# A hybrid decoder block on one core: the last weights' sums in quarter pieces, convolution taps queued behind products, other accumulator banks in mixing

## The chip, the cores and the metric

The kernel runs on one core of one Trainium2 chip. The time is the device time of one execution in microseconds (us), and the smaller the better. All engines are named as the profile names them: PE is TensorE (matmuls), DVE is VectorE, ACT is ScalarE, POOL is GpSimd, and SP is SyncE, which here issues all transfers (DMAs). Each engine works through its own instructions in order, and waits where one of them needs something of another engine or a transfer.

## The reference

One layer of a hybrid decoder block on 512 tokens of 1024 channels, in float32:

```
h = rmsnorm(x, norm1_g)
z_glu, z_rx, z_rg, z_ga, z_gb = split(h @ w_in + b_in)      # widths 2048, 1280, 1280, 1024, 1024
u  = z_glu[:, :1024] * sigmoid(z_glu[:, 1024:])
u  = causal_depthwise_conv(u, conv_dw_w, 31 taps)
ya = silu(layernorm(u)) @ conv_w_out + conv_b_out
xb = causal_depthwise_conv(z_rx, lru_conv_w, 4 taps)
hb = rg_lru(xb)                                             # gates in 16 blocks of 80, linear recurrence
yb = (hb * gelu(z_rg)) @ lru_w_out
x  = x + (sigmoid(z_ga) * ya + sigmoid(z_gb) * yb) @ w_mix_out
h  = rmsnorm(x, norm2_g)
x  = x + (silu(h @ ffn_w1) * (h @ ffn_w3)) @ ffn_w2         # width 2816
out = rmsnorm(x, norm_f_g)
```

## The kernel before

**Numbers and products.** Every float32 operand of a matmul is split into a high and a low part, and a product is three matmuls (high by high, high by low, low by high) into one accumulator. Three large products (mixing, the SwiGLU input, `ffn_w2`) are done in a seven-product form on 2x2 quarters, which needs sums of quarters of the weights and of the activations, and saves one matmul in eight. The weight sums (`t1` to `t4`) are made on the chip and stored in DRAM ahead of their use.

**Stages.** The first norm and its transposes; the input projection in tiles of 128 columns, in the hand-written order `ORDER`; the products `yb` and `ya`; mixing (`mxr`, L880); the second norm and its transposes (`th`); the SwiGLU input products for k = 0 to 10, of which k = 2 to 7 are the seven-product form (`ffn_seven`, `fr`, L1060: seven products of 24 matmuls of 128x256) and the others direct (`f`, L468: 24 matmuls of 128x512 a tile); the output product (`or`, L880); the final norm.

**Weight chunks.** All weights come in a fixed list of chunks of 128x1024 (`wchunk`, `emit_chunk`). Each chunk takes a `raws` tile (`RAW = 4` of them) for SP's load and an `hls` tile (5) for its parts; ACT casts the high part (L124) and DVE or POOL subtracts to get the low one (L120). `weights(key)` emits the chunks up to four ahead (`AHEAD = 4`) of the one that PE asks for. So the load of a chunk is issued when the chunk four before it was converted.

**The sums of `ffn_w2`.** For k = 0 and 1, POOL makes them during the input projection in half-column pieces (`o_piece` inside `make_f_sums`): two loads into one of three `wsums` tiles, four 128x256 operations, one store. For k = 2 to 10, `out_sums` calls `make_sums(k)` (L287) at the points of `OUT_SUMS`: it takes two of the four `raws` tiles, loads 512 KB into each, has DVE do four 128x512 operations (`ows`, L120 and L294), and stores them to DRAM (`ot<-ows`, L298). Its only rule of order is that it stands behind `turned`, the end of the second norm.

**Activation sums of the output product.** `Sevenfold.pair` makes the sums of one output pair (`ous`, `os`, `oe`, `ov`) on ACT and DVE. `release(keep)` does the pairs that are waiting, all but the last `keep`. The high and low parts `u_` of the first three pairs lie in `wsums` tiles (`PIECES`).

**The taps.** `beside` is a generator: each step is one tap of the 31-tap convolution on DVE (`cv`, L627), into a bank of accumulator memory; after the taps come ACT's copies `u`, then the layer norm's mean (`lnmt`, `lnms`, `lnmp`). `run_beside(n)` takes n steps after each tile of the projection. `rg(j)` is the tile of `z_rg`: Gelu on ACT (L785), the product with the recurrence's state on DVE (L786), and the split `y`. `gates(j)` (L733) makes the recurrence's coefficients; its operation `xb` at L760 reads the last of a gate's two banks.

**Banks.** Accumulator memory has eight banks: six in the pool `psum` (`bank`) and two in `psum2` (`bank2`). A tile gets a bank when its last reader is done. In `Sevenfold.run`, r1, r2, r5 and later r3 come from `bank`, r7 from `bank2`.

**Order.** The program order within an engine is chosen by a scheduler from the dependences and the order of the code. `tc.issue_after(x)` puts what it encloses behind instruction x; `manual_schedule` keeps the order written.

Of the kernel before, what the change touches and what calls it, by code (L numbers as in the profile page):

```python
# [1 line left out]

# [11 lines left out]
P = 128  # L14
T = 512
# [17 lines left out]
RAW = 4  # L33
HL = 5
AHEAD = 4
WARM = 12

FEW, MANY = 32, 112
# [49 lines left out]
def tile_block(ctx, tc, a, out):  # L88
# [53 lines left out]
    def emit_chunk():  # L142
        key, src, kt, cols, where, lo, after = chunks[emitted[0]]
        emitted[0] += 1
        n = kt * cols
        raw = raws.tile([P, 1024], F32, tag="raw", name=f"raw_{key}")
        rv = raw[:, :n]
        if callable(src):
            src(raw)
        else:  # L150
            newest["load"] = nc.sync.dma_start(rv.rearrange("p (k n) -> p k n", k=kt), src).ins
# [167 lines left out]
    def f_chunk(n, k):  # L319
        def load(raw_t):  # L320
            if n[0] == "t":
                nc.sync.dma_start(raw_t, f_sums[k][:, IN_PLACE.index(n), :])
            else:
                for i, w_ in enumerate((w1, w3)):
                    nc.sync.dma_start(raw_t[:, i * T : (i + 1) * T].rearrange("p (k n) -> p k n", k=4), f_quarter(n, k, w_, 0, 4))

        wchunk(f"f{n}_{k}", load, 8, P, lo=vec)

    def make_f_sums():

        def f_piece(k, i, c):
            four = (w1, w3)[i].rearrange("p (h k) (e n) -> p h k e n", h=2, e=2)
            at = T * i + P * c
            halves = [four[:, h, c : c + 2, :, k * P : (k + 1) * P].rearrange("p k e n -> p e k n") for h in range(2)]
            return f"{k}_{i}_{c}", halves, f_sums[k][:, :, at : at + 256]

        def o_piece(k, c):
            four = outq.w.rearrange("p (h k) (e n) -> p h k e n", h=2, e=2)
            cs = slice(256 * c, 256 * c + 256)
            return f"o{k}_{c}", [four[:, h, k, :, cs] for h in range(2)], outq.all_sums[k][:, :, cs]

        todo = [f_piece(k, i, c) for k in SEVEN for i in range(2) for c in (0, 2)]
        todo += [o_piece(k, c) for k in range(OUT_EARLY) for c in range(2)]
        sums_due, stores_due = [], []
        n, next_at = 0, SUMS_AT
        while todo or sums_due or stores_due:  # L350
            if stores_due and (emitted[0] >= stores_due[0][0] or not (todo or sums_due)):
                stores_due.pop(0)[1]()
            if sums_due and n >= sums_due[0][0]:
                sums_due.pop(0)[1]()
            if todo and n >= next_at:
                next_at += SUMS_STEP - (n >= SUMS_DENSE)
                name, halves, dest = todo.pop(0)
                raw = wsums.tile([P, 1024], F32, tag="wsum", name=f"fws{name}")
                q = [raw[:, 256 * m : 256 * m + 256] for m in range(4)]
                with tc.issue_after(newest["load"]):  # L360
                    for h, src in enumerate(halves):
                        to = raw[:, h * T : h * T + T]
                        to = to.rearrange("p (e k n) -> p e k n", e=2, k=2) if len(src.shape) == 4 else to.rearrange("p (e n) -> p e n", e=2)
                        nc.sync.dma_start(to, src)

                def sums(raw=raw, q=q, dest=dest):
                    q11, q12, q21, q22 = q
                    with tc.issue_after(newest["sub"]):
                        sub(pool_e, q22, q22, q12)
                        sub(pool_e, q12, q12, q11)  # L370
                        pool_e.tensor_tensor(out=q11, in0=q22, in1=q11, op=ALU.add)
                        sub(pool_e, q21, q21, q11)

                    def stores():
                        with tc.issue_after(newest["load"]):
                            nc.sync.dma_start(dest, raw.rearrange("p (m n) -> p m n", m=4))
# [406 lines left out]
    def rg(j):  # L783
        ps = in_mm(RG + j)
        act.activation(ps, ps, AF.Gelu_apprx_tanh, bias=b_in(RG + j))  # L785
        vec.tensor_tensor(out=ps, in0=hs[j], in1=ps, op=ALU.mult)  # L786
        y.append(split(f"y{j}", ps, vec))

    f_sums_steps = make_f_sums()
# [45 lines left out]
    class Sevenfold:  # L835
# [20 lines left out]
        def pair(self, k, ua, va):  # L856

            n = self.name

            p_ = None  # L860
            if n == "o" and k < PIECES:
                both = wsums.tile([P, 1024], F32R, tag="wsum", name=f"{n}us{k}")
                p_ = both[:, :T], both[:, T:]
            u_ = split(f"{n}us{k}", ua, vec, p_)
# [17 lines left out]
        def run(self, sums, begun, end):  # L882
# [71 lines left out]
    def mix_end(second, plus, r1, r2, r7, third):  # L954
# [11 lines left out]
        with tc.manual_schedule(engines={ET.PE, ET.Activation, ET.DVE}):  # L966
# [27 lines left out]


    o7 = Sevenfold(outq)
    sums_of = iter(range(OUT_EARLY, KF))

    def out_sums(n):

        with tc.issue_after(turned):
            for _ in range(n):
                k = next(sums_of, None)
                if k is not None:
                    outq.make_sums(k)

    def ffn_out(j, p1, p3):
        s_ = shortt(f"si{j}")
        act.activation(s_, p1, AF.Silu)
        o7.tile(j, lambda cs, dst: vec.tensor_tensor(out=dst, in0=s_[:, cs], in1=p3[:, cs], op=ALU.mult))  # L1010

    first_two = [0, KF]
    wf = [(w_tiles(f"f1_{j}", ND, 0), w_tiles(f"f3_{j}", ND, 0)) for j in first_two]
# [37 lines left out]
    def ffn_seven(k):  # L1051
# [12 lines left out]

        def out_of(c, dst):
            act.activation(c[:, LO], c[:, LO], AF.Silu)
            vec.tensor_tensor(out=dst, in0=c[:, LO], in1=c[:, HI], op=ALU.mult)
# [5 lines left out]
        product(r2, "a12", "b21")  # L1073
        add(c11, r2, c11)
        out_of(c11, u_[:, LO])
        product(r3, "s4", "b22")
        product(r1, "s2", "t2", True)
        q = shortt(f"q_{k}")
# [13 lines left out]
        product(r1, "a22", "t4", True)  # L1092
        add(c21, r1, c21)
        out_of(c21, v_[:, LO])
        o7.uv.append((u_, v_))
        o7.waiting.append((k, u_, v_))

    for k in range(1, KF):
        if k in SEVEN:
            ffn_seven(k)  # L1100
            out_sums(OUT_SUMS.get(k, 0))
            continue
        o7.release()
        for j in (k, k + KF):
            p1, p3 = bank(f"f1_{j}"), bank(f"f3_{j}")
            mm3(p1, w_tiles(f"f1_{j}", ND), h2)
            mm3(p3, w_tiles(f"f3_{j}", ND), h2)
            ffn_out(j, p1, p3)

            n_sums = OUT_SUMS.get(k, 0)  # L1110
            out_sums((n_sums + 1) // 2 if j < KF else n_sums // 2)
    assert next(sums_of, None) is None


    x2 = [[longt(f"x2b{t}{h}") for h in range(2)] for t in range(NT)]
# [10 lines left out]
    def finish(t, rest=None):  # L1126
# [82 lines left out]
```

## Time and profile before

| | us |
|---|---|
| median of 3 runs | 812.35 (811.15 to 812.42) |
| profiled execution, its own time | 814.2 |
| its span | 812.4 |
| PE busy | 796.9 |
| DVE, ACT, POOL busy | 659.1, 453.2, 255.1 |

The granted TensorE clock was 0.997 of full speed. The profile is of one execution, slower by 1.85 us than the median of the runs; 1.8 us of its time lie outside the span. PE is the engine with the most work, and the time can fall only where PE does not stand still any more. So the view to start with is that of PE's waits: who it waited for, how long in total, how often, and the longest. The views by time (stretches, the chain, the rows of an engine) give start, duration, engine, line, and "output <- inputs"; in square brackets stand the idle time before a row and what ended it.

### The profile page before, as it was taken

How to read it: one execution, taken by the hardware profiler on the slowest of the kernel's cores; microseconds unless marked ns; L12 is line 12 of the kernel's file. 1: busy time of each engine (PE TensorE's matmuls, PEld its weight loads, DVE VectorE, ACT ScalarE, POOL GpSimd, SP SyncE). 2: the span in 40 equal slices, each digit the busy share in tenths (PEclk: the TensorE clock that was granted, in tenths of full speed). 3: DMA queues.
4: the chain of work that ended last, by engine and by line, in shares of the span. 5: the costliest groups of instructions: out<-in, count | busy, mean ns of one | idle time of the engine just before them, and what ended most of it. 6: DMA issues, size and time to landing. Idle time of an engine off the chain costs nothing.

```text
span 812.4 us, 11845 instructions
## 1 busy us (share of the span) xinstructions
PE 796.9 (98%) x4182; PEld 687.1 (85%) x4182; DVE 659.1 (81%) x1018; ACT 453.2 (56%) x642; POOL 255.1 (31%) x204
## 2 busy tenths in 40 slices
PE   8999999999999999999999999998999999999996
PEld 7988888888887888888887898998999888888885
DVE  5699899998999989786799869878787866588556
ACT  7446688766687755653236454546464533476443
POOL 3475778766675866331310042000000000000000
PEclk9999999999999999999999999999999999999999
DMA  7645475766655663678888426778687888586552
GB/s 221 183 125 168 138 203 175 193 192 195 187 169 155 206 204 119 194 227 264 273 275 276 152 92 194 245 238 242 221 249 232 263 269 285 172 279 197 182 168 104
DMA packets 193839, 165.02 MB, mean 203 GB/s; under 512 B 12807, under 2 KB 164787, under 8 KB 193779
## 3 DMA queue, kind: packets, MB, share of 16 engines
q1 hardware_dynamic: 193779, 164.26, 66.4%
q8 instruction: 33, 0.54, 0.3%
q14 instruction: 27, 0.22, 0.1%
HBM read 130.80 MB, written 30.41 MB: 198 GB/s over the span
## 4 chain that ended last, share of the span: by engine, by line
PE 71%; DVE 12%; DMA 10%; issue 3%; ACT 2%; SPq 1%; POOL 1%; ACTq 0%; POOLq 0%; DVEq 0%
PE z L468 30%; PE or L880 13%; PE f L468 11%; PE fr L1060 10%; PE mxr L880 4%; DMA raw_co<-in_conv_w_out_dram 3%; DVE cv L627 2%; PE g L748 2%; DMA raw_in<-in_w_in_dram 2%; DMA raw_fb<-in_ffn_w_dram 1%; DMA ot<-ows 1%; DMA raw_lo<-in_lru_w_out_dram 1%; PE yb L468 1%; DVE hl_fb L120 1%; DMA ows<-in_ffn_w_dram 1%
## 5 line engine op out<-in xcount | busy, mean ns | idle before, releaser
L627 DVE SCALAR_TENSOR_TENSOR cv<-u,par,cv 128x511 f32<-128x511 f32 (+17 forms) x240 | 162.6, 729 | 1.1 <-ACT cv L624 0.9
L120 POOL TENSOR_TENSOR hl_in<-raw_in,hl_in 128x1024 fp32r<-128x1024 f32 x52 | 125.7, 2421 | 86.5 <-ACT hl_in L124 83.2
L120 POOL TENSOR_TENSOR fws<-fws 128x256 f32<-128x256 f32 x72 | 60.8, 846 | 30.9 <-DMA fws<-in_ffn_w_dram 27.7
L124 ACT CAST hl_in<-raw_in 128x1024 fp32r<-128x1024 f32 x52 | 54.2, 1042 | 6.3 <-PE z L468 3.0
L120 DVE TENSOR_TENSOR hl_ob<-raw_ob,hl_ob 128x1024 fp32r<-128x1024 f32 (+1 forms) x23 | 27.1, 1177 | 24.0 <-ACT hl_ob L124 23.9
L468 PE MATMUL z<-h10h,hl_in 128*128 128x512 f32 (+1 forms) x112 | 42.5, 381 | 2.2 <-DVE xb L760 1.4
L124 ACT CAST hl_ob<-raw_ob 128x1024 fp32r<-128x1024 f32 (+1 forms) x23 | 23.4, 1016 | 36.1 <-PE or L880 17.1
L468 PE MATMUL z<-h14h,hl_in 128*128 128x512 f32 (+1 forms) x112 | 41.7, 374 | 0.0
L468 PE MATMUL z<-h16h,hl_in 128*128 128x512 f32 (+1 forms) x112 | 41.7, 374 | 0.0
L468 PE MATMUL z<-h15h,hl_in 128*128 128x512 f32 (+1 forms) x112 | 41.7, 374 | 0.0
L468 PE MATMUL z<-h13h,hl_in 128*128 128x512 f32 (+1 forms) x112 | 41.7, 374 | 0.0
L468 PE MATMUL z<-h11h,hl_in 128*128 128x512 f32 (+1 forms) x112 | 41.7, 374 | 0.0
L468 PE MATMUL z<-h12h,hl_in 128*128 128x512 f32 (+1 forms) x112 | 41.7, 374 | 0.0
L468 PE MATMUL z<-h17h,hl_in 128*128 128x512 f32 (+1 forms) x112 | 41.7, 374 | 0.0
L124 ACT CAST hl_f<-raw_f 128x1024 fp32r<-128x1024 f32 x20 | 20.9, 1050 | 35.8 <-DMA raw_f<-in_ffn_w_dram 30.9
L120 DVE TENSOR_TENSOR hl_ft<-raw_ft,hl_ft 128x1024 fp32r<-128x1024 f32 x24 | 29.3, 1220 | 9.4 <-ACT hl_ft L124 9.4
L124 ACT CAST hl_ft<-raw_ft 128x1024 fp32r<-128x1024 f32 x24 | 24.9, 1048 | 19.4 <-DMA raw_ft<-fs 19.3
L1060 PE MATMUL fr<-hs_0h,hl_ft 128*128 128x256 f32 x192 | 35.5, 283 | 0.0
L120 DVE TENSOR_TENSOR hl_f<-raw_f,hl_f 128x1024 fp32r<-128x1024 f32 x20 | 26.7, 1341 | 10.8 <-ACT hl_f L124 10.7
L1060 PEld LDWEIGHTS fr<-hs_0h,hl_ft 128*128 128x128 f32 x192 | 30.4, 192 | 0.0
L120 DVE TENSOR_TENSOR hl_fb<-raw_fb,hl_fb 128x1024 fp32r<-128x1024 f32 x18 | 23.1, 1281 | 7.6 <-ACT hl_fb L124 7.6
L120 DVE TENSOR_TENSOR hl_ot<-raw_ot,hl_ot 128x1024 fp32r<-128x1024 f32 (+1 forms) x17 | 20.1, 1190 | 11.1 <-ACT hl_ot L124 10.7
(893 smaller groups left out, 2601.3 us busy)
## 6 DMA issues: line engine op xcount, KB each, us to landing
raw_in<-in_w_in_dram SPq DMA_DIRECT2D x52, 512.0 KB
fws<-in_ffn_w_dram SPq DMA_DIRECT2D x48, 256.0 KB
fs<-fws SPq DMA_DIRECT2D x24, 512.0 KB
raw_ft<-fs SPq DMA_DIRECT2D x24, 512.0 KB
raw_f<-in_ffn_w_dram SPq DMA_DIRECT2D x20, 512.0 KB
raw_fb<-in_ffn_w_dram SPq DMA_DIRECT2D x36, 256.0 KB
ows<-in_ffn_w_dram SPq DMA_DIRECT2D x18, 512.0 KB
ot<-ows SPq DMA_DIRECT2D x18, 512.0 KB
```

The costliest lines, as they stand in the source:

```text
L120: return eng.tensor_tensor(out=o, in0=x, in1=y, op=ALU.subtract)
L124: copy(h, full)
L468: pe.matmul(ps, l, r, start=i == 0, stop=i == n - 1)
L627: vec.scalar_tensor_tensor(out=acc[c][:, s:], in0=u[c][:, : T - s], scalar=dw(c, s), in1=acc[c][:, s:], op0=ALU.mult, op1=ALU.add)
L748: pe.matmul(ps, l, r, start=k == 0, stop=k == len(mms) - 1)
L880: pe.matmul(banks[i], l_[:, ts], r_, start=start and n == 0, stop=stop and n == 2, skip_group_check=again)
L1060: pe.matmul(ps[:, HALVES[i]], lw[:, 4 * i + c, :], rx_, start=not (again or i or c or m), stop=bool(i and c == 3 and m == 2), skip_group_c ...
```

## The change

Three edits, which do not touch what is computed, nor the order of PE's matmuls:

- **A.** The sums of `ffn_w2` for k = 2 to 10 are made in 18 half-column pieces through the `wsums` tiles, in place of nine whole sums through `raws` tiles. `out_step(k)` is called after a SwiGLU product three times in each `ffn_seven(k)` and four times in each direct k. Each call stores the piece whose sums were queued a call earlier, queues the sums of the piece loaded a call earlier (four 128x256 operations on DVE) behind the newest SwiGLU product, and, as `OUT_PIECES` says, loads the next piece; loads and stores stand behind the newest load issued. The first three pairs' `u_` move to the long-lived tiles. Pairs 5, 6 and 7 are left waiting until k = 8.
- **B.** From `rg(5)` on, each run of taps (`run_beside`) is queued on DVE behind the newest `rg` product (L786) that was there at the run before.
- **C.** In `Sevenfold.run`, r5 takes its banks from `bank2`, and r7 and r3 theirs from `bank`. The second norm's first transposes take turns between `bank` and `bank2`, and the final norm's unused squares go to `bank2`.

```diff
-OUT_SUMS = {1: 2, 2: 1, 4: 1, 6: 1, 7: 1, 8: 2, 9: 1}
+OUT_PIECES = {1: 3, 2: 1, 3: 2, 4: 1, 5: 2, 6: 1, 7: 2, 8: 3, 9: 3}
...
+    def piece_load(name, halves):
+        raw = wsums.tile([P, 1024], F32, tag="wsum", name=f"fws{name}")
+        for h, src in enumerate(halves):
+            to = raw[:, h * T : h * T + T]
+            to = to.rearrange("p (e k n) -> p e k n", e=2, k=2) if len(src.shape) == 4 else to.rearrange("p (e n) -> p e n", e=2)
+            nc.sync.dma_start(to, src)
+        return raw
+
+    def piece_sums(raw, eng):
+        q11, q12, q21, q22 = (raw[:, 256 * m : 256 * m + 256] for m in range(4))
+        sub(eng, q22, q22, q12)
+        sub(eng, q12, q12, q11)
+        eng.tensor_tensor(out=q11, in0=q22, in1=q11, op=ALU.add)
+        sub(eng, q21, q21, q11)
+
+    def piece_store(raw, dest):
+        nc.sync.dma_start(dest, raw.rearrange("p (m n) -> p m n", m=4))
...
+    behind = [None, None]
+
     def run_beside(n):
-        for _ in range(n):
-            next(side, None)
+        with tc.issue_after(behind[0]) if behind[0] else nullcontext():
+            for _ in range(n):
+                next(side, None)
+        behind[0] = behind[1] or behind[0]
...
-        vec.tensor_tensor(out=ps, in0=hs[j], in1=ps, op=ALU.mult)
+        product = vec.tensor_tensor(out=ps, in0=hs[j], in1=ps, op=ALU.mult)
+        behind[1] = product.ins if j >= BEHIND else None
...
-            r1, r2, r5 = ([bank(f"{n}{r}{i}") for i in range(2)] for r in ("r1", "r2", "r5"))
+            r1, r2 = ([bank(f"{n}{r}{i}") for i in range(2)] for r in ("r1", "r2"))
+            r5 = [bank2(f"{n}r5{i}") for i in range(2)]
...
-            r2, r7 = [bank(f"{n}r3{i}") for i in range(2)], [bank2(f"{n}r7{i}") for i in range(2)]
+            r7, r2 = ([bank(f"{n}{r}{i}") for i in range(2)] for r in ("r7", "r3"))
...
-                turn_half("th", xs, "norm2_g", h2p, 0, [bank], range(4 * q, 4 * q + 4))
+                turn_half("th", xs, "norm2_g", h2p, 0, [bank, bank2], range(4 * q, 4 * q + 4))
...
+    out_todo = [o_piece(k, c) for k in range(OUT_EARLY, KF) for c in range(2)]
+    out_at, out_quota = [None, None], dict(OUT_PIECES)
+
+    def out_step(k):
+        if out_at[1]:
+            with tc.issue_after(newest["any"]):
+                piece_store(*out_at[1])
+        if out_at[0]:
+            with tc.issue_after(newest["now"]):
+                piece_sums(out_at[0][0], vec)
+        out_at[1], out_at[0] = out_at[0], None
+        if out_quota.get(k, 0):
+            out_quota[k] -= 1
+            name, halves, dest = out_todo.pop(0)
+            with tc.issue_after(newest["any"]):
+                out_at[0] = piece_load(name, halves), dest
...
-        o7.release(max(0, k - 6))
+        o7.release({6: 1, 7: 3}.get(k, 0))
...
-        r = rstd_of([x2[t][h], x2[t][1 - h]], [bank(f"jk{t}{i}") for i in range(2)], between)
+        r = rstd_of([x2[t][h], x2[t][1 - h]], [bank2(f"jk{t}{i}") for i in range(2)], between)
```

More of the change, by code (lines that the diff above doesn't have):

```diff
@@ L1 @@
-from contextlib import ExitStack
+from contextlib import ExitStack, nullcontext
 import concourse.bass as bass
@@ L35 @@
 AHEAD = 4
+BEHIND = 5
 WARM = 12
@@ L150, in emit_chunk @@
         else:
-            newest["load"] = nc.sync.dma_start(rv.rearrange("p (k n) -> p k n", k=kt), src).ins
+            newest["load"] = newest["any"] = nc.sync.dma_start(rv.rearrange("p (k n) -> p k n", k=kt), src).ins
         if where == "hl":
@@ L321, in load @@
             if n[0] == "t":
-                nc.sync.dma_start(raw_t, f_sums[k][:, IN_PLACE.index(n), :])
+                newest["any"] = nc.sync.dma_start(raw_t, f_sums[k][:, IN_PLACE.index(n), :]).ins
             else:
                 for i, w_ in enumerate((w1, w3)):
-                    nc.sync.dma_start(raw_t[:, i * T : (i + 1) * T].rearrange("p (k n) -> p k n", k=4), f_quarter(n, k, w_, 0, 4))
+                    newest["any"] = nc.sync.dma_start(raw_t[:, i * T : (i + 1) * T].rearrange("p (k n) -> p k n", k=4), f_quarter(n, k, w_, 0, 4)).ins
@@ L327, in f_chunk, with f_piece @@
         wchunk(f"f{n}_{k}", load, 8, P, lo=vec)
-    def make_f_sums():
[L335 to L344, printed above, removed]
+    def f_piece(k, i, c):
+        four = (w1, w3)[i].rearrange("p (h k) (e n) -> p h k e n", h=2, e=2)
+        at = T * i + P * c
+        halves = [four[:, h, c : c + 2, :, k * P : (k + 1) * P].rearrange("p k e n -> p e k n") for h in range(2)]
+        return f"{k}_{i}_{c}", halves, f_sums[k][:, :, at : at + 256]
@@ new lines, in o_piece @@
+    def o_piece(k, c):
+        four = outq.w.rearrange("p (h k) (e n) -> p h k e n", h=2, e=2)
+        cs = slice(256 * c, 256 * c + 256)
+        return f"o{k}_{c}", [four[:, h, k, :, cs] for h in range(2)], outq.all_sums[k][:, :, cs]
+    def piece_load(name, halves):
[5 more added lines that the diff above has]
+        return raw
@@ L357, in make_f_sums, with sums @@
                 name, halves, dest = todo.pop(0)
-                raw = wsums.tile([P, 1024], F32, tag="wsum", name=f"fws{name}")
-                q = [raw[:, 256 * m : 256 * m + 256] for m in range(4)]
                 with tc.issue_after(newest["load"]):
[L361 to L367, printed above, removed]
+                    raw = piece_load(name, halves)
+                def sums(raw=raw, dest=dest):
                     with tc.issue_after(newest["sub"]):
[L369 to L372, printed above, removed]
+                        piece_sums(raw, pool_e)
                     def stores():
                         with tc.issue_after(newest["load"]):
-                            nc.sync.dma_start(dest, raw.rearrange("p (m n) -> p m n", m=4))
+                            piece_store(raw, dest)
                     stores_due.append((emitted[0] + STORE_LAG, stores))
@@ L858, in pair @@
             n = self.name
[L860 to L864, printed above, removed]
+            u_ = split(f"{n}us{k}", ua, vec)
             s1 = shortt(f"{n}s1{k}")[:, LO]
@@ L996, in tile_block @@
     o7 = Sevenfold(outq)
[L997 to L1005, printed above, removed]
+    out_todo = [o_piece(k, c) for k in range(OUT_EARLY, KF) for c in range(2)]
[13 more added lines that the diff above has]
+                out_at[0] = piece_load(name, halves), dest
     def ffn_out(j, p1, p3):
@@ L1009, in ffn_out, with make @@
         act.activation(s_, p1, AF.Silu)
-        o7.tile(j, lambda cs, dst: vec.tensor_tensor(out=dst, in0=s_[:, cs], in1=p3[:, cs], op=ALU.mult))
+        def make(cs, dst):
+            newest["now"] = vec.tensor_tensor(out=dst, in0=s_[:, cs], in1=p3[:, cs], op=ALU.mult).ins
+        o7.tile(j, make)
     first_two = [0, KF]
@@ L1066, in out_of @@
             act.activation(c[:, LO], c[:, LO], AF.Silu)
-            vec.tensor_tensor(out=dst, in0=c[:, LO], in1=c[:, HI], op=ALU.mult)
+            newest["now"] = vec.tensor_tensor(out=dst, in0=c[:, LO], in1=c[:, HI], op=ALU.mult).ins
         r1, r2, r3, r5, r7 = bank(f"fr1_{k}"), bank2(f"fr2_{k}"), bank(f"fr3_{k}"), bank2(f"fr5_{k}"), bank(f"fr7_{k}")
@@ L1094, in ffn_seven @@
         out_of(c21, v_[:, LO])
+        out_step(k)
         o7.uv.append((u_, v_))
@@ L1106, in tile_block @@
             mm3(p1, w_tiles(f"f1_{j}", ND), h2)
+            out_step(k)
             mm3(p3, w_tiles(f"f3_{j}", ND), h2)
             ffn_out(j, p1, p3)
-            n_sums = OUT_SUMS.get(k, 0)
-            out_sums((n_sums + 1) // 2 if j < KF else n_sums // 2)
-    assert next(sums_of, None) is None
+            out_step(k)
+    assert not out_todo and out_at == [None, None]
     x2 = [[longt(f"x2b{t}{h}") for h in range(2)] for t in range(NT)]
```

3 lines of the change are left out of this document (2 added, 1 removed).

## The prediction

> **What bounds the kernel now.** I read the page first, then who TensorE (PE) waits for, then a table of stretches.
>
> ```profile
> span 812.4 us, 11845 instructions
> PE 796.9 (98%) x4182; PEld 687.1 (85%) x4182; DVE 659.1 (81%) x1018; ACT 453.2 (56%) x642; POOL 255.1 (31%) x204
> ```
>
> PE is busy for 796.9 of 812.4 us, so a change that leaves the matmuls alone can win at most the 15.5 us in which PE stands still. Part of that is the start and the tail, which this change does not touch. The view of PE's waits names the rest:
>
> ```profile
> PE fr L1060 <- ACT q L1079: 2.1, 1, 2.1
> PE z L468 <- DVE xb L760: 1.4, 1, 1.4
> ...
> PE mxr L880 <- DVE sga L937: 0.8, 1, 0.8
> ```
>
> Three single waits, one for each part of the change: 2.1 in the SwiGLU products, 1.4 in the input projection, 0.8 in mixing, together 4.3 us. The table of stretches says where nothing is lost:
>
> ```profile
> 520.00:540.00 20.00, 20.00 (x169) 20.00 (x168) 14.78 (x23) 9.81 (x14) 0.00 (x0) 1.00 0.80 236
> 540.00:560.00 20.00, 17.91 (x149) 17.71 (x149) 14.10 (x20) 9.69 (x13) 0.00 (x0) 1.00 0.88 259
> 560.00:580.00 20.00, 20.00 (x169) 20.00 (x168) 17.79 (x29) 11.74 (x18) 0.00 (x0) 1.00 0.72 217
> ```
>
> The first number pair is PE. It is full in two of these, at a granted clock of 1.00 (third number from the end), and lacks 2.09 us in 540 to 560. So each part is worth its own wait, and no more.
>
> **Part A, sums of the last weights in quarter pieces.** The chain of waits explains the 2.1 us:
>
> ```profile
> 539.92 3.00 DMA ot<-ows
> ...
> 542.93 0.38 SPq L325
> ...
> 543.37 6.38 DMA raw_fb<-in_ffn_w_dram
> ...
> 549.85 1.04 ACT hl_fb L124
> 550.89 0.49 ACT q L1079
> ...
> 551.43 0.62 PE fr L1060 x3
> ```
>
> Whole sums live in the `raws` tiles of the weight chunks: two of four. The load of chunk `fb` needs such a tile, so it was issued at 542.93, when the store `ot<-ows` (3.00) was through. It landed at 549.75; ACT, which works in order, did its cast (1.04) and only then the copy `q` that frees the accumulator for PE's next product.
>
> ```profile
> 549.06 0.28 PE L1060 MATMUL fr<-hs_1h,hl_ft 128*128 128x256 f32 x1
> 551.43 0.39 PE L1060 MATMUL fr<-h24h,hl_ft 128*128 128x256 f32 x1 [2.08 <-ACT q L1079]
> ```
>
> Start to start 2.37 us, and 0.12 is normal (the 169 matmuls of the full stretches in 20 us; this one lacks 20): 2.25 are lost. With the pieces in `wsums` tiles the chunk loads have all four `raws` tiles, and no chunk load waits for a store's landing to get a buffer. How far ahead the chunks then are, two rows of before show:
>
> ```profile
> 592.42 1.23 DVE L120 TENSOR_TENSOR hl_fb<-raw_fb,hl_fb 128x1024 fp32r<-128x1024 f32 x1 [3.66 <-ACT hl_fb L124]
> ...
> 608.42 1.23 DVE L120 TENSOR_TENSOR hl_fb<-raw_fb,hl_fb 128x1024 fp32r<-128x1024 f32 x1 [0.17 <-ACT hl_fb L124]
> ```
>
> ```profile
> 594.72 0.28 PE L1060 MATMUL fr<-h20h,hl_fb 128*128 128x256 f32 x1
> ...
> 617.76 0.28 PE L1060 MATMUL fr<-h24h,hl_fb 128*128 128x256 f32 x1
> ```
>
> The first chunk, loaded beside a sum, was ready at 593.65 for a product at 594.72: 1.07 us of slack. The second, with no sum near, at 609.65 for 617.76: 8.1. Part A should move the chunks towards the second. Gain: 2.1 to 2.25.
>
> What A adds. DVE: 36 operations of 128x512 become 72 of 128x256.
>
> ```profile
> L120 DVE TENSOR_TENSOR ows<-ows,ows 128x512 f32<-128x512 f32 x18 | 12.3, 686 | 10.3 <-DMA ows<-in_ffn_w_dram 10.2
> L120 DVE TENSOR_TENSOR oe<-ou,ov 128x256 f32<-128x256 f32 x20 | 8.3, 417 | 0.0
> ```
>
> 72 x 0.417 - 36 x 0.686 = 30.0 - 24.7 = 5.3 us more of DVE time, spread over some 200 us. I cost it at nothing: DVE is idle for 5.2, 5.9 and 2.2 us in the three stretches from 520 to 580. If that cover were gone, each microsecond would first eat chunk slack. [...]
>
> DMA: the bytes stay, each sum's runs go from 4 KB to 1 KB, and SP issues 36 loads and 18 stores for 18 and 18, so 18 issues more at 0.38: 6.8 us of SP over 200. Small runs could cost engine time:
>
> ```profile
> q1 hardware_dynamic: 193779, 164.26, 66.4%
> ```
>
> ```profile
> q1 hardware_dynamic: 4152, 5.15, 86.6%
> ```
>
> The first row is the whole run (mean packet 848 bytes), the second 540 to 560 (1240 bytes). 16 x 812.4 x 0.664 / 164.26 = 52.5 us of engine time for a MB, and 16 x 20 x 0.866 / 5.15 = 53.8: smaller packets were no dearer, so the bounds are -1.3 and +1.3 us a MB, and I take nothing. [...]
>
> SP works in order too: the store of a piece waits for its sums on DVE, which are queued behind the newest SwiGLU product. SP runs ahead of PE by about the 8.1 us of slack, so it will be held at stores for some microseconds. The next chunk load is then late against today's undisturbed ones, but starts from 8 us of slack and four buffers. Pairs 5 to 7 are left for the direct products from k = 8, where DVE's queue gets them behind chunks needed soon. I cost both at nothing.
>
> **Part B, taps behind products.** DVE's order decides this one:
>
> ```profile
> 244.19 0.66 ACT L785 ACTIVATE z<-z,par 128x512 f32<-128x512 f32 x1
> ...
> 244.87 5.97 DVE L627 SCALAR_TENSOR_TENSOR cv<-u,par,cv 128x511 f32<-128x511 f32 x9
> ...
> 250.75 0.68 DVE L786 TENSOR_TENSOR z<-xb,z 128x512 f32<-128x512 f32 x1
> ...
> 251.47 0.59 ACT L124 CAST y5h<-z 128x512 fp32r<-128x512 f32 x1 [5.64 <-DVE z L786]
> ...
> 256.58 0.39 PE L468 MATMUL z<-h17l,hl_in 128*128 128x512 f32 x1
> 256.80 0.39 PE L468 MATMUL z<-h17h,hl_in 128*128 128x512 f32 x1
> ...
> 257.89 0.68 DVE L760 SCALAR_TENSOR_TENSOR xb<-g,xb 128x512 f32<-128x512 f32 x1
> ...
> 258.63 0.50 PE L468 MATMUL z<-h10h,hl_in 128*128 128x512 f32 x1 [1.44 <-DVE xb L760]
> ```
>
> The Gelu was done at 244.85, but DVE did nine taps (5.97) before product `z`, and ACT stood 5.64 behind it. The next PE tile needs the bank that `xb` at L760 frees. After the change the product stands ahead of the nine taps, so ACT's chain and `xb` come up to 5.9 us earlier, against 1.44 that are needed. PE's start-to-start step is 1.83 here, normal is 0.22 to 0.23 (256.58 to 256.80): gain 1.4 to 1.6. What is late next: the taps after the last products. Their end feeds the layer norm's mean:
>
> ```profile
> 310.20 1.16 DVE L120 TENSOR_TENSOR lnmsl<-lnmt,lnmsh 128x512 fp32r<-128x512 f32 x1 [0.69 <-ACT lnmsh L124]
> ```
>
> ```profile
> 313.39 0.39 PE L638 MATMUL lnmp<-lnmsl,onesr 128*128 128x512 f32 x1
> ```
>
> That is ready at 311.36, and PE takes it 2.0 us later (313.39). PE comes 1.6 earlier, so 0.4 are left. Later taps could use that up; I take no loss here and keep 0 to 1.6 for the rivals.
>
> **Part C, other banks in mixing.**
>
> ```profile
> 426.09 0.39 PE L880 MATMUL mxr<-mxt10h,mxs1p 128*128 128x512 f32 x1
> ...
> 426.48 0.74 DVE L937 SCALAR_TENSOR_TENSOR sga<-ya,par,sga 128x512 f32<-128x512 f32 x1
> ...
> 427.27 0.50 PE L880 MATMUL mxr<-mxt10h,mxs1p 128*128 128x512 f32 x1 [0.79 <-DVE sga L937]
> ```
>
> Product r5's second bank is the one of the last `ya`, which DVE reads until 427.22. Taken from the two banks that the layer norm left free, it waits for nothing: 1.18 start to start less 0.23, gain 0.8 to 0.95. What is late next is DVE, which does not come earlier with PE:
>
> ```profile
> 440.36 0.69 DVE L825 TENSOR_TENSOR x<-mxr,x 128x512 f32<-128x512 f32 x1
> ...
> 442.37 0.61 PE L880 MATMUL mxr<-hl_mxt,mxvb0h 128*128 128x512 f32 x2
> ```
>
> r1's second bank is read until 441.05 and written again at 442.37, after the change at 441.4: 0.4 us left.
>
> **Sum.** 2.1 + 1.4 + 0.8 = 4.3 by the waits, 2.25 + 1.6 + 0.95 = 4.8 start to start; I take the middle, 4.55. The profiled execution took 814.2 (span 812.4 and 1.8 around it), so 809.65. The median of the runs lies 1.85 lower, at 812.35: **807.8**.
>
> **Rivals.** *R1, A's wait returns.* SP, held at a piece's store, issues a chunk load as late as at 542.93, and ACT again meets the cast before `q`. Against: four buffers and 8 us of slack. For: k = 3, 5 and 7 each have two pieces, with DMA at 0.72 to 0.88 already. Each return costs up to 2.25; at two of these k: 809.65 + 4.5 - 1.85 = 812.3.
>
> *R2, B does not do what it says, or is given back.* DVE idles ahead of a product that waits for ACT, the taps come out late by what they were meant to win, and PE waits at the layer norm's mean. Then 1.6 comes back: 809.4; with C's 0.95 lost in the same way 810.35.
>
> *R3, slower: DVE is held by pieces that land late.* DVE works in order, and behind a piece's sums are queued the subtraction of the next weight chunk and the next product's evacuation.
>
> ```profile
> DVE ows L120 <- DMA ows<-in_ffn_w_dram: 10.2, 5, 3.6
> ```
>
> DVE waited five times for today's sums, 2.04 us on average. If each of the nine pieces issued in k = 2 to 7 holds DVE for 2.04 while chunks stand as tight as at 594.72 (1.07), PE loses 0.97 nine times, 8.7: 809.65 + 8.7 - 1.85 = 816.5. It beats the gain from a hold of 0.5 past the slack each time. Against: a piece gets a whole step (two or three products of 24 x 0.12 = 2.88 us) between load and sums, and the slack should grow. For: landings of 6.38 are longer than two products.
>
> **How the numbers follow.** Forecast 0.58, R1 0.13, R2 0.14, R3 0.15. A measurement of this kernel can tell about 0.2%, 1.6 us: faster is below 810.7, slower above 814.0. Forecast and R2 are faster: 0.72. R1 is the same: 0.13. R3 is slower: 0.15. The forecast's own range is 807.5 to 808.1, and with the spread of the runs (811.15 to 812.42 about 812.35) 806.4 to 808.9. With R1 and R2 it reaches to 812.4, which leaves R3's 0.15 out.
>
> **What would show it.** In the profile after, PE's waits lack the three rows above and have no new one over 0.5; 540 to 560 shows PE at 20.00; product `z` stands right behind its Gelu on DVE, and chunks in k = 3 and 4 are ready 5 us or more ahead of PE. R1 would show as `q` or `c` behind an ACT cast, R2 as PE waiting for `lnms` or `x`, R3 as PE waiting for `hl_f`, `hl_ft` or `hl_fb` while DVE waits for `fwso`. A new wait in the output product, where quick loads count, would make the prediction wrong in a way that I have not priced.

## The result and the profile after

The changed kernel took 809.26 us in the median of six runs (808.08 to 809.93), the one before 812.38 in six runs beside it (811.15 to 815.14). The ratio is 0.9955, with a 95% interval of 0.9938 to 0.9972: faster by 0.45%, some 3.7 us, or 3.1 by the medians. The forecast was 807.8, 4.55 below before: right in sign, and about a microsecond too much in size. The number alone would not tell why. 809.26 lies just above the forecast's own range (806.4 to 808.9) and next to the 809.4 of rival R2. The waits below tell the two apart: under R2 PE would wait for `xb` still, at the layer norm's mean, or for `x` in mixing, and it does none of these. Two of the three terms came, and the third was not there to be won.

The profiled execution of the changed kernel took 808.5, with a span of 806.6. First the page and PE's waits of the changed kernel (us in total, times, longest):

```profile
span 806.6 us, 11905 instructions
PE 795.6 (99%) x4182; PEld 687.4 (85%) x4182; DVE 660.2 (82%) x1054; ACT 455.4 (56%) x643; POOL 254.3 (32%) x204
```

```profile
PE par_ps L462 <- DMA rows<-in_b_in_dram: 1.8, 1, 1.8
PE warm L450 <- DVE ones L443: 1.1, 1, 1.1
PE tx L518 <- DVE x L534: 0.7, 1, 0.7
PE f L478 <- ACT h20h L521: 0.3, 1, 0.3
PE z L478 <- POOL hl_in L121: 0.2, 1, 0.2
```

The three waits for `q`, `xb` and `sga` are gone and no new one over 0.5 is there; what is left lies in the first 10 us, but for the 0.2 for a weight chunk at 25.75 and the 0.3 at the second norm. The table of stretches has the same three rows that the prediction showed, now all full for PE:

```profile
520.00:540.00 20.00, 20.00 (x169) 20.00 (x168) 16.08 (x24) 10.76 (x15) 0.00 (x0) 1.00 0.98 304
540.00:560.00 20.00, 20.00 (x169) 20.00 (x169) 17.21 (x30) 11.15 (x16) 0.00 (x0) 1.00 0.88 269
560.00:580.00 20.00, 20.00 (x169) 20.00 (x168) 16.91 (x27) 10.98 (x16) 0.00 (x0) 1.00 0.85 273
```

DMA (second number from the end; before 0.80, 0.88 and 0.72) is as busy as before or more, and it does not matter, since the chunks are far ahead. A chunk of k = 4 on DVE, and the product that uses it on PE:

```profile
544.81 1.22 DVE L121 TENSOR_TENSOR hl_fb<-raw_fb,hl_fb 128x1024 fp32r<-128x1024 f32 x1
```

```profile
554.46 0.28 PE L1086 MATMUL fr<-hs_1h,hl_fb 128*128 128x256 f32 x1
```

Ready at 546.03 for 554.46: 8.4 us of slack, where before the chunks of k = 3 and 4 had 2.3 to 5.8. Of the whole k = 3 to 7 the smallest is now 5.6; in k = 2 it is 2.8, against 2.4 before.

What SP waited for from 505 to 700 us shows the mechanism of part A itself. Before, four chunk loads of line L325 stood for the landing of a sum's store, 9.5 us in all. After, no chunk load does, only the pieces' own loads (L346). First before, then after:

```profile
SPq L325 <- DMA ot<-ows: 9.5, 4, 3.4
```

```profile
SPq L346 <- DMA ot<-fwso: 5.0, 4, 2.0
```

In the projection, product `z` stands right behind its Gelu (ends 244.59), ahead of the taps, and `xb` comes at 251.72, six us earlier than before:

```profile
243.93 0.66 ACT L801 ACTIVATE z<-z,par 128x512 f32<-128x512 f32 x1
...
244.62 0.70 DVE L802 TENSOR_TENSOR z<-xb,z 128x512 f32<-128x512 f32 x1
245.22 1.41 DVE L637 SCALAR_TENSOR_TENSOR cv<-u,par,cv 128x511 f32<-128x511 f32 x2
...
251.72 0.68 DVE L776 SCALAR_TENSOR_TENSOR xb<-g,xb 128x512 f32<-128x512 f32 x1
```

### The profile page after: what moved, and what is told of

It reads as the page before. It is cut to its first block, busy times and chain, and to the rows that moved or that the text cites. A ratio compares the mean times of both kernels' runs of the same rounds, so it can differ in the third digit from the quotient of the medians.

```text
span 806.6 us, 11905 instructions
## 1 busy us (share of the span) xinstructions
PE 795.6 (99%) x4182; PEld 687.4 (85%) x4182; DVE 660.2 (82%) x1054; ACT 455.4 (56%) x643; POOL 254.3 (32%) x204
## 3 DMA queue, kind: packets, MB, share of 16 engines
q1 hardware_dynamic: 207891, 164.26, 67.0%
## 4 chain that ended last, share of the span: by engine, by line
PE 96%; DMA 1%; SPq 1%; DVE 0%; POOL 0%; ACT 0%; issue 0%
PE z L478 34%; PE fr L1086 15%; PE f L478 14%; PE or L892 13%; PE yb L478 7%; PE ya L478 5%; PE mxr L892 5%; PE g L764 3%; DMA raw_in<-in_w_in_dram 1%; SPq L434 1%; PE th L518 0%; SPq L427 0%; POOL hl_in L121 0%; DVE of L1159 0%; ACT hl_in L125 0%
## 5 line engine op out<-in xcount | busy, mean ns | idle before, releaser
L125 ACT CAST hl_f<-raw_f 128x1024 fp32r<-128x1024 f32 x20 | 20.9, 1050 | 34.2 <-PE f L478 19.6
L125 ACT CAST hl_fb<-raw_fb 128x1024 fp32r<-128x1024 f32 x18 | 18.9, 1050 | 18.5 <-PE fr L1086 7.1
```

What stands on the lines that cost most here:

```text
L125: copy(h, full)
```

## The experiments

All kernels were timed beside the kernel before on the same chip. Theory: three separate waits, which add up, and of part A the buffers. Rivals: the parts give back in one place what they win in another; and in A it is the size or the queues of the pieces, not the buffers.

**Each part alone.**

For A alone (e1), the changed kernel has these lines taken back, and the other banks of C with them; B alone (e2) and C alone (e3) are the kernel before with the lines of that part; e4 is the changed kernel itself.

```diff
-        behind[1] = product.ins if j >= BEHIND else None
...
-            r1, r2 = ([bank(f"{n}{r}{i}") for i in range(2)] for r in ("r1", "r2"))
-            r5 = [bank2(f"{n}r5{i}") for i in range(2)]
+            r1, r2, r5 = ([bank(f"{n}{r}{i}") for i in range(2)] for r in ("r1", "r2", "r5"))
```

> Only part A (quarter pieces through their own buffers, the pairs left until k = 8) on the kernel before; taps and banks as before. Theory (three separate waits that add up): PE's wait for the copy q (2.1) is gone, the waits for xb (1.4) and sga (0.8) stay; the time is 2.1 to 2.3 us below before, about 810.1. Rival (the parts lean on each other, a wait won in one place comes back in another): with the earlier waits kept, PE meets another wait of over 0.5 us in the SwiGLU products, and the time is within 1 us of before.

> Only part B (taps behind the products from rg(5) on) on the kernel before. Theory: the wait for xb (1.4) is gone, the waits for sga (0.8) and q (2.1) stay as they are; 1.4 to 1.6 us below before, about 810.8. Rival: DVE's work was only put off, and PE waits at the layer norm's mean (lnms) or for sga longer than 0.8, so that at most 0.5 us is left.

> Only part C (r5 from the two banks of the layer norm, r7 and r3 from the six) on the kernel before. Theory: the wait for sga (0.8) is gone, the waits for xb and q stay; 0.8 to 0.95 us below before, about 811.5, which the rounds can hardly tell from nothing, so the trace decides. Rival: DVE is full from 426 to 447 and does not come earlier, so PE waits for an addition to x by as much as it won, and no gap is smaller in sum.

> The changed kernel once more, beside the three single parts on one chip. Theory: the three gains add, 4.3 to 4.8 us below before. In the first measurement it was 3.1 by the medians, and the two profiled executions differ by 5.7 in their own times. If the difference is the spread of single executions, this one should lie between 3 and 5 again, and the sum of the three single parts within 1.5 us of it. Rival: the parts give something back that the trace of one execution does not show, and the sum of the three parts is clearly above what all together give.

Measured, as ratios to before (812.27 in 26 runs), each with its interval, and the medians:

| | median | ratio | 95% interval |
|---|---|---|---|
| A alone | 810.37 | 0.9973 | 0.9963 to 0.9983 |
| B alone | 810.57 | 0.9982 | 0.9970 to 0.9993 |
| C alone | 813.21 | 1.0006 | 0.9996 to 1.0016 |
| all | 808.56 | 0.9959 | 0.9946 to 0.9971 |

A is worth 2.2 us (0.27%), B 1.5 (0.18%), C nothing that can be measured: by its interval it gains 0.3 us at most. The three add to 0.39%, all together give 0.41%: these intervals show nothing that is given back, and the forecast's terms for A (2.1 to 2.25) and B (1.4 to 1.6) agree with them. They are wide, though: 1.4 to 3.0 us for A and 0.6 to 2.4 for B. The term for C does not agree. PE's waits of A alone and of B alone say more, since both have the old banks. A alone:

```profile
PE z L478 <- DVE xb L776: 1.0, 1, 1.0
...
PE f L478 <- ACT h20h L521: 0.3, 1, 0.3
PE g L764 <- DMA ext6l<-xb7l: 0.2, 1, 0.2
```

B alone:

```profile
PE fr L1066 <- ACT q L1085: 1.4, 1, 1.4
...
PE f L469 <- ACT h20h L512: 0.3, 1, 0.3
```

Neither has a wait for `sga`. So the 0.8 that the first profile showed there was not the banks' price in every execution. That gave the new theory for C: a wait of one execution, in which DVE was late.

**The kernel before, once more.** No edit.

> The kernel before, looked at once more. Theory (part C's wait belonged to one execution, in which two loads of mixing came late and DVE with them): PE's waits for q (about 2) and xb (0.3 to 1.5) are there again, the one for sga is not, or smaller. Rival (the banks cost 0.8 in every execution, and parts A and B alone won it by some other way): the wait for sga is there again with 0.8.

It took 811.96 (one run). PE's waits:

```profile
PE fr L1060 <- ACT q L1079: 1.6, 1, 1.6
...
PE z L468 <- DVE xb L760: 0.9, 1, 0.9
```

`q` and `xb` are there again, `sga` is not. DVE's last operation on `sga`, in this execution:

```profile
422.52 0.75 DVE L937 SCALAR_TENSOR_TENSOR sga<-ya,par,sga 128x512 f32<-128x512 f32 x1 [0.54 <-PE ya L468]
```

Here DVE was idle and waited for PE's `ya`; in the first profile of before the same operation began at 426.48, with no idle time before it. There DVE had fallen behind at two chunks that came late:

```profile
404.87 1.79 DVE L120 TENSOR_TENSOR hl_co<-raw_co,hl_co 128x1024 fp32r<-128x1024 f32 x1 [0.71 <-ACT hl_co L124]
...
408.11 1.23 DVE L120 TENSOR_TENSOR hl_co<-raw_co,hl_co 128x1024 fp32r<-128x1024 f32 x1 [0.78 <-ACT hl_co L124]
```

In the execution of C alone neither of these two waits is in the rows, and DVE had caught up by then. So the cause, a DVE late by two late chunks, is seen in one execution; that a late DVE suffices, the next two kernels show.

**A DVE made late, with the old banks (e10) and the new (e11).** The additions stand ahead of the last of the eight operations on `sga`; their result is used by nothing.

```diff
-        vec.scalar_tensor_tensor(out=o, in0=ps, scalar=pc("conv_b_out", j), in1=o, op0=ALU.add, op1=ALU.mult)
+        last = None
+        if n == 7:
+            extra = shortt("extra")
+            for _ in range(7):
+                last = add(extra, sga[3], sga[3])
+        with tc.issue_after(last.ins) if last else nullcontext():
+            vec.scalar_tensor_tensor(out=o, in0=ps, scalar=pc("conv_b_out", j), in1=o, op0=ALU.add, op1=ALU.mult)
```

> The kernel before with seven additions of 128x512 that nothing uses (7 x 0.61 = 4.3 us) on DVE ahead of its last operation on sga. Theory (C is a guard against a late DVE): PE waits for sga 2 to 3.5 us at product r5, where DVE was on time it waited not at all. Rival (DVE's lateness is caught elsewhere): no wait for sga over 1 us.

> The same seven additions, with part C's banks. Theory: no wait for sga; 1.5 to 3.5 us less of PE's waits than with the old banks and about the time of the kernel before, as long as PE does not need the last mxus before DVE has it (5 us later in the row). Rival (DVE is the bound there anyway): PE waits as long a few products later, for mxus or x, and both kernels take the same time.

The old banks took 818.04 (ratio 1.0065, 1.0049 to 1.0082), the new ones 812.77 (1.0001, 0.9989 to 1.0013). Old banks:

```profile
430.15 0.74 DVE L943 SCALAR_TENSOR_TENSOR sga<-ya,par,sga 128x512 f32<-128x512 f32 x1
430.95 0.80 PE L880 MATMUL mxr<-mxt10h,mxs1p 128*128 128x512 f32 x1 [3.94 <-DVE sga L943]
```

New banks:

```profile
425.24 0.62 PE L880 MATMUL mxr<-mxt10h,mxs1p 128*128 128x512 f32 x2
425.69 0.39 PE L880 MATMUL mxr<-mxt10l,mxs1p 128*128 128x512 f32 x1
425.92 0.39 PE L880 MATMUL mxr<-mxt10h,mxs1p 128*128 128x512 f32 x1
...
428.32 0.75 DVE L944 SCALAR_TENSOR_TENSOR sga<-ya,par,sga 128x512 f32<-128x512 f32 x1
```

With the old banks r5's second half waits 3.94, a little more than expected; with the new ones PE has done it before DVE gets to `sga`, and only 0.7 comes back later, as a wait for `x`. By the medians the two kernels are 5.3 us apart, more than the 1.5 to 3.5 expected; part of that is a stretch of lower clock right behind the wait of 3.94, which the last section shows. So C is cover for a late DVE: with `sga` six us or more later than in the second profile of before (430.15 and 428.32 against 422.52) it spares PE most of a wait of 3.94, and where DVE is on time it buys nothing.

**What carries part A.** Five kernels take its ingredients apart. e5, the pieces of `out_step` in the chunks' buffers:

```diff
+    late = [False]
+
     def piece_load(name, halves):
-        raw = wsums.tile([P, 1024], F32, tag="wsum", name=f"fws{name}")
+        raw = (raws if late[0] else wsums).tile([P, 1024], F32, tag="raw" if late[0] else "wsum", name=f"fws{name}")
...
+    late[0] = True
```

e6, `make_sums` and `OUT_SUMS` as before, but in own buffers, with B, C and the late pairs of the changed kernel:

```diff
-            q = [raws.tile([P, 1024], F32, tag="raw", name=f"{self.name}ws{k}_{i}") for i in range(2)]
+            q = [(raws if self.parts else wsums).tile([P, 1024], F32, tag="raw" if self.parts else "wsum", name=f"{self.name}ws{k}_{i}") for i in range(2)]
```

e7, the same three times in `out_step`, for stores, sums and loads:

```diff
-            with tc.issue_after(newest["any"]):
+            with tc.issue_after(turned):
```

e8, the sums in the step of their load:

```diff
-        if out_at[0]:
-            with tc.issue_after(newest["now"]):
-                piece_sums(out_at[0][0], vec)
-        out_at[1], out_at[0] = out_at[0], None
+        out_at[1] = None
...
             with tc.issue_after(newest["any"]):
-                out_at[0] = piece_load(name, halves), dest
+                out_at[1] = piece_load(name, halves), dest
+            with tc.issue_after(newest["now"]):
+                piece_sums(out_at[1][0], vec)
```

e12, whole sums, each in two `wsums` tiles and begun when the last is stored, queued as in the changed kernel:

```diff
-    out_todo = [o_piece(k, c) for k in range(OUT_EARLY, KF) for c in range(2)]
+    out_todo = list(range(OUT_EARLY, KF))
...
+        if out_todo and not out_at[1]:
+            kk = out_todo.pop(0)
+            with tc.issue_after(newest["any"]):
+                q = [wsums.tile([P, 1024], F32, tag="wsum", name=f"ows{kk}_{i}") for i in range(2)]
+                for i, v in enumerate(q):
+                    nc.sync.dma_start(v, outq.w[:, kk + KF * i, :])
+            out_at[0] = q, kk
```

> The changed kernel, but the quarter pieces of k = 2 to 10 lie in the four raws tiles of the weight chunks, one tile for each piece; size, places and queues as changed. Theory (it was the buffers: a sum that holds chunk buffers makes a chunk load late): the chunks' slack ahead of PE in k = 3 to 7 falls from 6 to 9 us to under 4 in places, DMA-bound waits of PE of 1 us or more come back in the SwiGLU products, and the time is 1.5 to 4 us above the changed kernel. Rival (it was the size and the place of the pieces): no wait of PE over 0.5 us, the time within 0.7 us of the changed kernel.

> The changed kernel, but with whole sums as before (two loads of 512 KB, four 128x512 operations, 4 KB runs, behind the second norm only, at the old places), in two of the three wsums tiles in place of two raws tiles. Theory (buffers): no wait of PE in the SwiGLU products, slack of 6 us or more, the time within 0.7 us of the changed kernel. Rival (size and place): a wait for q or its like of 1 us or more stays, the time 1 to 2.5 us above the changed kernel.

> The changed kernel, but the pieces' loads, sums and stores stand only behind the end of the second norm, not behind the newest load or SwiGLU product. Theory (buffers): no wait of PE over 0.5 us, the time within 1 us of the changed kernel. Rival (the queues matter: a store ahead of its place holds SP, sums ahead of their load hold DVE): DVE waits for fwso for some us in sum, the chunks' slack falls below 3, and PE waits; 1 to 5 us above the changed kernel.

> The changed kernel, but a piece's sums are queued on DVE in the same step as its load, not a step later. This prices the third rival of the prediction: DVE held by a piece that has not landed, with the next weight chunk's subtraction and the next product behind it. Theory: DVE waits for fwso in many of the 18 places, up to 5 us each, but the chunks are some 8 us ahead, so PE waits little: 0 to 4 us above the changed kernel. Rival (what hangs on DVE is not the chunk but the SwiGLU product, which frees PE's accumulators and has no such slack): PE waits in most k, 8 us or more above the changed kernel.

> The changed kernel with whole sums in two of the three own buffers, but with the changed kernel's queues: store behind the newest load, sums behind the newest SwiGLU product and a step after their load, a new sum only when the last is stored. It leaves the size alone as the difference. Theory (buffers and queues carry part A, quarters only make it fit): no wait for hs, c or q over 0.7 us, the time within 1 us of the changed kernel. Rival (size: a sum needs two tiles at once, so its load stands on SP until the store before it has landed, and the chunk loads behind it): chunks' slack falls below 4 us, and PE waits 1 to 5 us in all.

| | buffers | size | queues | median | ratio to before (95%) |
|---|---|---|---|---|---|
| changed (e4) | own | quarter | placed | 808.56 | 0.9959 (0.9946 to 0.9971) |
| e8 | own | quarter | placed, no step between | 808.27 | 0.9955 (0.9942 to 0.9968) |
| e6 | own | whole | free | 814.47 | 1.0024 (1.0013 to 1.0035) |
| e7 | own | quarter | free | 816.93 | 1.0063 (1.0049 to 1.0078) |
| e12 | own | whole | placed | 817.89 | 1.0071 (1.0056 to 1.0086) |
| e5 | chunks' | quarter | placed | 826.04 | 1.0181 (1.0166 to 1.0196) |

These runs come from three chips, so compare by the ratios, each to the kernel before on its own chip. My theory that the buffers alone carry A fell. The buffers are needed (e5 is 17 us above the changed kernel, far over the 4 that I gave as the most), but with own buffers and either of the other two left out, the kernel is slower than before: e6, e7 and e12 are 5.9, 8.4 and 9.3 us above the changed kernel, more than any of the expectations had.

*e5.* A piece keeps one of four chunk buffers from its load to its store's landing. The slack of most chunks in k = 2 to 7 falls to between -1.2 and 3 us. On SP, from 505 to 700 us, chunk loads stand for a piece's store again, on this line four times:

```profile
SPq L326 <- DMA ot<-fwso: 6.1, 4, 2.6
```

PE's waits:

```profile
PE fr L1089 <- ACT q L1109: 3.8, 3, 1.5
PE fr L1089 <- DVE hl_ft L121: 3.1, 6, 0.8
PE or L894 <- ACT si L1034: 3.0, 1, 3.0
PE fr L1089 <- ACT c L1101: 1.8, 2, 1.7
```

*e6 and e7, free queues.* With own buffers, nothing but the second norm holds the sums back, so they go ahead of the SwiGLU's own inputs `hs` on DVE. PE's waits in e7:

```profile
PE fr L1086 <- ACT hs_1h L125: 2.7, 1, 2.7
PE fr L1086 <- ACT c L1098: 1.2, 1, 1.2
PE fr L1086 <- DVE hs_1l L121: 1.2, 1, 1.2
```

All three fall in k = 2, between 518 and 525. From 470 to 720 us DVE waited five times for a piece that had not landed, 5.0 us in all, as the rival said; but the chunks' slack from k = 3 on stays at 4.8 or more, so it was `hs` that came late and not the chunks. In the kernel before, the chunks' buffers were the brake as well: a sum could only begin when two of them were free. e6 also shows the mechanism of my third rival at a place of its own. Its profiled execution, 817.94, is the slowest of its twelve (812.18 to 817.94), so the waits shown here are those of a bad case. DVE, then PE:

```profile
576.09 0.69 DVE L121 TENSOR_TENSOR ows<-ows,ows 128x512 f32<-128x512 f32 x1 [4.82 <-DMA ows<-in_ffn_w_dram]
576.70 0.68 DVE L831 TENSOR_TENSOR q<-fr,q 128x512 f32<-128x512 f32 x1
577.30 1.22 DVE L121 TENSOR_TENSOR hl_fb<-raw_fb,hl_fb 128x1024 fp32r<-128x1024 f32 x1
```

```profile
585.37 0.39 PE L1062 MATMUL fr<-hs_0h,hl_ft 128*128 128x256 f32 x1 [2.28 <-ACT c L1074]
```

DVE stands 4.82 before a sum whose load is late, with an addition that frees an accumulator and a chunk queued behind it; the chain of waits leads from that load through DVE's queue to ACT's copy `c`, for which PE waits 2.28 nine us later. In the changed kernel DVE waits for no piece at all from k = 1 on.

*e8.* Load and sums in one step cost nothing (0.9955 against 0.9959), and DVE waits for no piece there either, where waits of up to 5 us had been expected. So e8 does not price the third rival. SP is far enough ahead: a piece whose load was issued at 542.94 had its sums begun at 556.75, behind a product of the same step.

*e12.* Whole sums need two of three tiles at once, so a new load stands on SP until the store before it has landed (nine times from 505 to 640, 14.7 us in all), and a store until its sums are done, with the chunk loads behind them. SP's rows:

```profile
545.71 2.06 SPq L1018 DMA_DIRECT2D ot<-ows  x2
547.87 0.45 SPq L326 DMA_DIRECT2D raw_fb<-in_ffn_w_dram  x1
```

SP issued nothing between 541.37 and 545.71, where this store waited for its sums; chunk `fb22` of k = 4 was ready at 557.01, 1.2 us after PE had begun the product that uses it, and PE waited 0.93 and 0.75 there. The smallest slacks of k = 4 to 7 lie between -1.2 and 1. Size therefore matters, through the number of tiles that a sum holds. But size is not the only difference that e12 leaves, as its expectation says it is: it begins a sum as soon as the last is stored and issued its last sum load at 606.7, where the changed kernel spreads its pieces until 659.4. How much of the 9.3 us is size and how much the denser schedule is not shown.

## Why the prediction was right, point by point

- **The bound.** That PE's stalls are what there is to win is borne out for the most part. PE's idle time fell from 15.5 to 11.0 us, and its busy time from 796.9 to 795.6: together the 5.8 us by which the span shrank. The 1.3 cannot be put down to the change, since PE's busy time differs by as much between executions (797.0 in e9, 794.9 in B alone).
- **A, 2.1 to 2.25.** 2.2 by itself, with an interval of 1.4 to 3.0. The exact match is partly luck: 2.1 too is the wait of one execution, and in five others with the old sums (e2, e3, e9, e10, e11) `q` cost 1.4 to 1.8. The reason was only half right. That no chunk load waits for a sum's buffer any more is shown on SP, and e5 shows what it costs where they do. But "SP held at stores", which I cost at nothing, is cheap only because the pieces are small or spread out (e12) and queued (e7). "Pairs left until k = 8" cost nothing in the changed kernel, where PE has no wait in the output product; no kernel tests them by themselves.
- **DVE's extra time.** Shown: the 72 piece operations take 21.9 + 7.4 = 29.3 us, 30.0 was the estimate, and the stretches keep PE full. The estimate was even too high: operations in a row overlap, with starts 0.34 us apart (the third row below: four in 1.43) and 0.60 for whole ones (e6's rows above), so what DVE has to do in addition is nearer 72 x 0.34 - 36 x 0.60 = 2.9 us than 5.3. Half the elements cost DVE more than half the time (417 ns for 128x256, 686 for 128x512 before), but that decides nothing here: e12 keeps the 512 elements and is 9 us slower than the changed kernel. The rows of the changed kernel:

```profile
L121 DVE TENSOR_TENSOR fwso<-fwso 128x256 f32<-128x256 f32 x54 | 21.9, 417 | 0.1
L353 DVE TENSOR_TENSOR fwso<-fwso 128x256 f32<-128x256 f32 x18 | 7.4, 415 | 0.0
```

```profile
508.97 1.43 DVE L121 TENSOR_TENSOR fwso<-fwso 128x256 f32<-128x256 f32 x4
```

- **DMA.** q1's packets rose from 193779 to 207891 for the same 164.26 MB, and its share of the engines, of a span 0.7% shorter, from 66.4% to 67.0%: as good as no price for shorter runs, as taken. The issue on SP was mis-sized: 0.60 for a piece's load and 0.57 for its store, where 0.38 was used, so SP has some 20 us more to do (36 x 0.60 + 18 x 0.57 - 36 x 0.34 = 19.6), not 6.8. It is hidden all the same. Issue times of the pieces' loads on SP (ns, least, median, most):

```profile
L346 SPq DMA_DIRECT2D fwso<-in_ffn_w_dram x44: 545/603/1917, 359.1 to 659.4; - x44
```

- **B, 1.4 to 1.6.** 1.5 by itself, with an interval of 0.6 to 2.4, so the size is only roughly shown; in five other executions with the old taps the wait was 0.3 to 1.2 (last section). The mechanism is shown by the rows of product `z` and `xb` above. That the layer norm's mean would have 0.4 us left was wrong, on the safe side. In the changed kernel DVE is ready at 307.35 and PE takes it at 311.39, 4.0 us later:

```profile
306.19 1.16 DVE L121 TENSOR_TENSOR lnmsl<-lnmt,lnmsh 128x512 fp32r<-128x512 f32 x1 [0.69 <-ACT lnmsh L125]
```

  DVE no longer stands idle ahead of the last product `z` (2.63 us before), and the mean's first addition begins at 296.20 in place of 299.07, so nothing was put off.
- **C, 0.8 to 0.95.** This is the step that failed. "Product r5's second bank ... waits for nothing: gain 0.8 to 0.95" took a wait of one profiled execution for one of every execution. Alone C gives a ratio of 1.0006 (0.9996 to 1.0016), and a second profile of the kernel before has no such wait. What stands in its place is 0 for a DVE on time, and 3.94 for one made late.
- **The offset to the median.** I took 1.85 us off the profiled execution's time and left all its waits in the sum. Part of what made that execution slow was such waits: PE was idle for 15.5 us there and for 13.2 in e9, with `q` and `xb` 0.5 longer each and `sga` 0.8. Without C's term, which stood in the sum with the middle of 0.8 and 0.95, the forecast is 3.7 below before, and the ratio 0.9955 says 3.7. That match has luck in it: the waits of e9 for `q` and `xb` make 1.6 + 0.9 = 2.5. The upper end of the forecast's range, 808.9, does not follow from the spread that it names either, which gives 808.1 + 0.07 = 808.2.
- **The rivals.** R1 and R3 did not come. Both are real where something of part A is left out: in e5 PE waits for `q` behind late chunks again (R1), and in e6 DVE is held by a late sum and PE pays (R3). R2 did not come: C's gain is missing, but because the wait is not there in most executions, not because it came back elsewhere.

What stays open: why in one execution the two chunks of mixing came late, and how often that happens; what the pairs cost by themselves; and how e12's loss divides between size and schedule. The price of C was set by lateness made on purpose, not by counting executions.

## What to carry to other kernels

A wait that one profile shows once is worth its size only if a second profile shows it again; a second profile of the kernel before, at the price of one run, would have set C's term to zero. Work that is moved to buffers of its own loses the brake that the shared buffers were, so the new place needs its order written down (without it e7 is 8.4 us above the changed kernel), and pieces small enough that none of them holds an in-order queue (with whole sums, and their denser schedule, e12 is 9.3 above). Where an engine that works in order has to do side work, put it behind the operation that others wait for: that alone gave B its 1.5 us, with not one instruction less.

## What the runs showed of the hardware that I had not expected

- The wait for `xb` was the shorter, the more time PE had lost ahead of it. In six executions with the old taps (before twice, e1, e3, e10, e11) it was 1.4, 1.2, 1.0, 0.9, 0.9 and 0.3 us, and PE's wait for the transfer `ext6l`, 75 us earlier, was 0, 0, 0.2, 0.2, 0.2 and 0.6. It looks as if DVE set the later point in time, so that what PE loses earlier costs nothing; no run delays PE there on purpose, so this is argued from six executions.
- A piece's load took longer to issue on SP than a whole sum's, though the bytes are half: 0.34 us in the median for 512 KB in 4 KB runs (`ows`, before), 0.60 for 256 KB in 1 KB runs (`fwso`, after). That the length of the runs is the reason is not shown by itself.
- A wait of PE went with a loss beyond its own length. In e10 the granted clock behind the wait of 3.94 is 0.70 over five us and then 1.00 again, and PE's matmuls start 0.43 us apart for a while in place of 0.23; from 0.70 over five us the loss is an estimated 1.5 us. In the rows the first pair is PE, and the third number from the end is the clock:

```profile
431.00:436.00 5.00, 5.00 (x16) 4.01 (x17) 4.25 (x9) 1.54 (x3) 0.00 (x0) 0.70 0.76 210
436.00:441.00 5.00, 5.00 (x24) 4.14 (x23) 1.58 (x2) 1.97 (x3) 0.00 (x0) 1.00 1.02 367
```

  e6, e7 and e12 have five such microseconds each at 0.66 (from 585, 520 and 557), behind waits in the SwiGLU products. The kernels before and after have no stretch of 20 us below 1.00 between 20 and 800. A long wait is not always followed by it: e5's 2.97 at 713 is not, so when it comes is not shown.
